# One hybrid decoder layer on one core: v's transposes and the first state-space unit later, the first norm's root on token columns, GELU on ACT and DVE, the last tiles by halves

## Chip, cores and metric

The kernel runs on one core of a Trainium2 chip, as one program. The metric is the device time of that core in microseconds, the median of several executions. The profile shows one execution: its span goes from the first to the last instruction that is recorded, and its own time is 1.8 us more than the span.

## What is computed

One inference step of one layer, for a prompt of 512 tokens and 8 single tokens of a sample group, which makes T = 520 columns of D = 1024 features:

```python
h = rmsnorm(x, g_mix)
z = h @ w_in          # u (512) | SWA q, k, v | three dilated q, k, v | three gates (3 x 1024)
a = gelu_glu(ssm(u))                    # branch A: complex diagonal state space, 32 groups x 64 states
b = banded_attention(q, k, v, sink)     # branch B
c = dilated_attention(...)              # branch C: keys by strides 1, 4, 16
x = x + (sigmoid(g_a) * (a @ w_a) + sigmoid(g_b) * (b @ w_b) + sigmoid(g_c) * (c @ w_c)) @ w_out
x = x + relu(rmsnorm(x) @ w_up) ** 2 @ w_down
x = x + sigmoid(rmsnorm(x) @ w_pg) * (p @ w_pp)
y = rmsnorm(x)
```

All of it is in float32. The new key and value rows and the state of the state space are outputs too. The change leaves this as it is; GELU is the form with tanh, in which `y (1 + 0.044715 y^2)` is now written as `0.044715 y (1 / 0.044715 + y^2)`.

## The kernel before

**Projections.** The activations lie transposed: features in partitions (8 tiles of 128, k = 0 to 7), tokens in columns, cut into half 0 (columns 0 to 255) and half 1 (256 to 519: 264 columns). One tile f of a projection is 128 output features; for each half it is a *half tile* of 24 matmuls, since float32 is rebuilt from three passes in fp32r for each k: high weight by high activation (`wh`, `hh`, L282), high by low (`hl`, L283), low by high (`wl`, L284). `load_w` brings a weight in pieces of 256 KB with a DMA of SyncE's queue (SP, L267); ACT rounds it to `wh` (L270) and DVE subtracts to get `wl` (L271). Four `wh` and `wl` slots and five raw ones are in turn; a weight can only be rounded when the piece four before has been used for the last time. `load_w` has a second set of two slots for a pool of its own, used for `w_pp`. PSUM has a ring of three `mm` banks and four `aux` banks, and single banks `stat` and `saux`.

**Order.** Each engine runs its own queue in order. The program is written as one sequence, which a scheduler then rearranges within its dependencies. Where in the sequence side work stands is set by *lanes*: after each half tile `tick()` lets every lane take a step (class `Lane`). Lane 0 computes the state space's parameters (`ssm_steps`: many small DVE and POOL operations, at the end eight pairs of tables `a2`, the powers, L618 to L626, each sent to `esc` by a DMA). The lane `att` holds attention and the transposes of v, `ssml` the eight units of the state space. A unit has eleven stages, in which `None` is an empty one: loads, tables (POOL computes X and others, L729 to L743), inputs, blocks (PE L761 and L763 on X), turned, windows, chunks, scan, None, states, outputs (to DRAM). The second argument of the lane is the gap: a unit begins five ticks after the one before.

**The stretches the change touches.** *Start*: SP issues x's parts and the first two weights in turn (`take`, W01); ACT makes `hh` (L347) and the squares of x (L417). `first_norm` sums the squares over features with a matmul with ones (L450), one column for each token in all 128 partitions, and `inverse` forms 1/sqrt on tiles of 128x256 and 128x264: ACT's root (L367) and five DVE operations (L368 to L372), the reciprocal among them. Each projection is multiplied by this when it is evacuated (`u` L678 and L679, `qkv` L877 to L882). *v_tokens* (L890) transposes v, 128x128 a time, in the step after its projection. *GELU*: in the branch b, at tiles f = 2 to 5, y comes from DRAM; POOL forms y + 0.044715 y^3 in three operations (L1369 to L1371), ACT takes the tanh (L1372), DVE multiplies (L1373, L1376), ACT and DVE split the product (`gh` L292, `gl` L296). *End*: the last product is the gate's. `tiles` hands out the half tiles as `TURNS` lists them; here the last four are (6, 1), (7, 1), (6, 0), (7, 0), each 24 matmuls and 6 of `w_pp`. DVE forms x (L1487, L1488), ACT its square (L307) and the scaled copy `yo` (L1493). After f = 7 of a half comes the final norm: sums on token columns (L340), for half 1 `newton` (three DVE operations, then twelve of POOL, L355 to L362), for half 0 a root on ACT and `root_inverse` (L367 to L372). `spread` turns the columns to rows: diagonals `nd` (L1497 by ACT, L1501 by DVE), a matmul with ones (L389) and a copy (L391). DVE and POOL multiply `yo` by it (L1506, L1504), and DMAs take it out (L1508). A table load on ACT (L1491) gets the square root back in the last tile.

Of the kernel before, what the change touches and what calls it, by code (L numbers as in the profile page):

```python
# [10 lines left out]
F32 = mybir.dt.float32  # L11
# [187 lines left out]
def body(tc, nc, I, O):  # L199
# [61 lines left out]
    def load_w(src, nk, pool=None, ks=None, lo_by=None):  # L261
        out = []
        pl, sfx, nb = (wp, "", 4) if pool is None else (pool, "p", 2)
# [87 lines left out]
    def newton(ps, n, on):  # L351

        nt = ev.tile([128, 4, 3], F32, name="nt", bufs=2)[:, :, :n]
        v, w, y, t = (nt[:, i] for i in range(4))
        V.tensor_scalar(v, ps, 1.0 / D, EPS, op0=OP.mult, op1=OP.add)  # L355
        V.tensor_scalar(y.bitcast(I32), v.bitcast(I32), -0.5, float(0x5f3759df), op0=OP.mult, op1=OP.add)
        V.tensor_scalar(w, v, -0.5, None, op0=OP.mult)
        for _ in range(3):
            on.tensor_tensor(t, w, y, op=OP.mult)
            on.tensor_tensor(t, t, y, op=OP.mult)  # L360
            on.tensor_scalar(t, t, 1.0, 1.5, op0=OP.mult, op1=OP.add)
            on.tensor_tensor(y, t, y, op=OP.mult)  # L362
        return y
# [17 lines left out]
    def spread(y, half, on):  # L381

        pr = stat()
# [45 lines left out]
    for k0, n, w in ((0, 2, 0), (2, 2, 4), (4, 4, None)):  # L429
        do = take(0, k0, n)  # L430
        if w is not None:
            W01[0] += load_w(I["w_in"][0], 8, ks=[w])
        do()
    for k0 in (0, 4):
        do = take(1, k0, 4)
        W01[1] += load_w(I["w_in"][1], 8, ks=[k0])
        do()
# [8 lines left out]
    def first_norm():  # L446
        for half, bank_ in enumerate((stat, aux)):
            c0, c1 = HALVES[half]
            ps = bank_()[:, :c1 - c0]
            PE.matmul(ps, ones, sq0[:, 0, c0:c1], start=True, stop=True)  # L450
            Rr[half] = inverse(ps)
# [238 lines left out]
    def ssm_sub(s):  # L690
# [145 lines left out]
        ssml.add(loads, tables, inputs, blocks, turned, windows, chunks, scan, None, states, outputs)  # L836
# [152 lines left out]
    def dilated(gi, f0, perm, name, Vt, i):  # L989
# [6 lines left out]
        att.add(v_tokens(Vt[i], v))  # L996
# [187 lines left out]
    for i in (4, 5, 0, 1, 2, 3):  # L1184
# [3 lines left out]
        if i == 5:  # L1188
            Vs = qt("vs")[:, 0:512].rearrange("p (b c) -> p b c", b=4)
            att.add(v_tokens(Vs, ts[5]))  # L1190
# [172 lines left out]
    def gelu(f):  # L1363
        def do():
# [4 lines left out]
            G.tensor_tensor(t, y, y, op=OP.mult)  # L1369
            G.tensor_scalar(t, t, 0.044715, 1.0, op0=OP.mult, op1=OP.add)  # L1370
            G.tensor_tensor(t, t, y, op=OP.mult)  # L1371
            A.activation(t, t, AF.Tanh, scale=math.sqrt(2.0 / math.pi))  # L1372
# [44 lines left out]
    def tiles(load, swap=False):  # L1417
        for t in TURNS:
            if swap and len(t) == 4:
                t = [(f, 1 - half) for f, half in t]  # L1420
# [62 lines left out]
    for f, half, (W, Wy) in tiles(lambda f: (load_w(I["w_pg"][f], 8), load_w(I["w_pp"][f], 2, pe)), swap=True):  # L1483
# [5 lines left out]
        if (f, half) == (7, 0):  # L1489

            A.activation(pe.tile([128, 1], F32, name="root"), t[:, 0:1], AF.Sqrt, scale=0.0, bias=ones[:, 0:1])  # L1491
        add_square(x, f, half, A, True, wide=False)
        A.activation(yo[:, f, c0:c1], x[:, f, c0:c1], AF.Copy, scale=prm[:, P_GF + f:P_GF + f + 1])  # L1493
        if f == 7:
            n = len(starts(half))
            if half:
                r, pr_ = spread(newton(ssp_[half][:, :n], n, G), half, lambda d, i, y: A.activation(d, i, AF.Copy, scale=y))  # L1497
            else:
                nt = ev.tile([128, 3, 2], F32, name="nr", bufs=1)
                y = root_inverse(ssp_[half][:, :n], *(nt[:, i] for i in range(3)))  # L1500
                r, pr_ = spread(y, half, lambda d, i, y: V.tensor_scalar(d, i, y, None, op0=OP.mult))  # L1501
            for k in range(8):
                if k in ((1, 2, 3, 5, 7) if half else (2, 5, 7)):
# [3 lines left out]
                if k % 2:  # L1507
                    (nc.sync if k in (1, 5) else nc.scalar).dma_start(O["yT"][:, k - 1:k + 1, c0:c1], yo[:, k - 1:k + 1, c0:c1])  # L1508
# [42 lines left out]
```

## Time and profile before

| | before |
|---|---|
| median of 3 runs | 1007.12 us (1006.59 to 1007.61) |
| profiled execution, its own time | 1006.62 us |
| its span | 1004.8 us |
| mean granted TensorE clock | 0.986 of full |
| PE busy (matmuls) | 974.3 us, 97% |
| PEld, weight loads, beside PE | 938.4 us, 93% |
| DVE busy | 622.0 us, 62% |
| ACT busy | 380.4 us, 38% |
| POOL busy | 247.3 us, 25% |

How to read it: the share of PE is an average; 30.5 us of its span are idle, in few places. The granted clock is the share of TensorE's full clock that the chip gave; it has two levels, 1.00 (2.4 GHz) and 0.50 (1.2 GHz), and a mean between them says how a stretch is divided. A busy PE at the lower level is busy for longer with the same work.

### The profile page before, as it was taken

Reading aid. Unit: us, or ns where it says so; the run is one execution under the profiler, and the core shown is the slowest. Engines: PE = TensorE matmul, PEld = TensorE weight load, DVE = VectorE, ACT = ScalarE, POOL = GpSimd, SP = SyncE. Lnnn points to the kernel's source line nnn. Section 1 sums busy time; section 2 is a strip of 40 time slices with the busy share of each in tenths; the row PEclk is TensorE's granted clock in tenths of the full one; section 3 lists DMA queues with packets and bytes.
Section 4 is the critical chain, followed back from the end, with each engine's and each line's share of the span. In section 5 each row is a group of like instructions: output and inputs, shape, how many; then the busy total and the mean of one; then the engine's idle time right before and its main releaser. Section 6 shows DMA issues by size and latency. Waiting matters only on the chain.

```text
span 1004.8 us, 20850 instructions
## 1 busy us (share of the span) xinstructions
PE 974.3 (97%) x8076; PEld 938.4 (93%) x8076; DVE 622.0 (62%) x1489; ACT 380.4 (38%) x845; POOL 247.3 (25%) x392
## 2 busy tenths in 40 slices
PE   7988899999999999999999999999999999999994
PEld 7988789988788999999999999999999999999994
DVE  7998556565988585566666844533543444366863
ACT  6323233342445443353344533322332233145652
POOL 0267855545531062100000132300320121000003
PEclk9999899999999999999999999999999999999997
DMA  6536544346322153352332232232232232232402
GB/s 227 174 107 205 150 120 127 97 117 190 117 70 62 50 153 95 93 170 86 95 105 86 85 102 88 91 99 86 93 98 85 95 95 84 85 106 86 147 12 85
DMA packets 80051, 108.46 MB, mean 108 GB/s; under 512 B 20432, under 2 KB 35920, under 8 KB 79952
## 3 DMA queue, kind: packets, MB, share of 16 engines
q1 hardware_dynamic: 78144, 105.64, 33.7%
q10 hardware_dynamic: 1808, 1.49, 0.5%
q8 instruction: 63, 1.03, 0.4%
q14 instruction: 36, 0.29, 0.1%
HBM read 97.04 MB, written 10.07 MB: 107 GB/s over the span
## 4 chain that ended last, share of the span: by engine, by line
PE 84%; DVE 6%; POOL 4%; DMA 2%; ACT 2%; issue 1%; POOLq 0%; SPq 0%; DVEq 0%
PE mm L282 21%; PE mm L284 21%; PE mm L283 21%; PE aux L282 4%; PE aux L284 4%; PE aux L283 4%; PE aux L906 2%; PE aux L931 1%; PE aux L964 1%; DVE wl L271 1%; PE aux L1240 1%; PE saux L827 1%; PE saux L828 1%; PE saux L788 1%; DMA bct<-bc 1%
## 5 line engine op out<-in xcount | busy, mean ns | idle before, releaser
L282 PE MATMUL mm<-hh,wh 128*128 128x256 f32 (+1 forms) x1072 | 306.7, 286 | 4.3 <-ACT wh L270 3.5
L284 PE MATMUL mm<-hh,wl 128*128 128x256 f32 (+1 forms) x1072 | 304.9, 285 | 0.2 <-DVE wl L271 0.2
L283 PE MATMUL mm<-hl,wh 128*128 128x256 f32 (+1 forms) x1072 | 304.2, 284 | 0.4 <-DVE hl L348 0.4
L270 ACT ACTIVATE wh<-wr 128x512 fp32r<-128x512 f32 (+1 forms) x292 | 181.2, 624 | 309.1 <-PE mm L283 243.4
L271 DVE TENSOR_TENSOR wl<-wr,wh 128x512 fp32r<-128x512 f32 (+1 forms) x290 | 210.5, 727 | 131.2 <-ACT wh L270 123.3
L282 PEld LDWEIGHTS mm<-hh,wh 128*128 128x128 f32 x1072 | 202.8, 189 | 8.1 <-ACT wh L270 3.8
L284 PEld LDWEIGHTS mm<-hh,wl 128*128 128x128 f32 x1072 | 203.1, 189 | 2.3 <-issue 1.8
L283 PEld LDWEIGHTS mm<-hl,wh 128*128 128x128 f32 x1072 | 203.0, 189 | 2.0 <-issue 1.4
L282 PE MATMUL mm<-rh,wh 128*128 128x256 f32 (+1 forms) x512 | 144.9, 283 | 0.0
L284 PE MATMUL mm<-rh,wl 128*128 128x256 f32 (+1 forms) x512 | 144.6, 282 | 0.0
L283 PE MATMUL mm<-rl,wh 128*128 128x256 f32 (+1 forms) x512 | 144.4, 282 | 0.0
L1450 POOL TENSOR_TENSOR e<-e 128x256 f32<-128x256 f32 x64 | 54.9, 859 | 350.1 <-DVE e L1449 279.5
L282 PE MATMUL aux<-hh,wh 128*128 128x264 f32 (+1 forms) x400 | 115.7, 289 | 1.6 <-ACT wh L270 1.6
L284 PE MATMUL aux<-hh,wl 128*128 128x264 f32 (+1 forms) x400 | 114.3, 286 | 0.6 <-DVE wl L271 0.6
L283 PE MATMUL aux<-hl,wh 128*128 128x264 f32 (+1 forms) x400 | 113.8, 285 | 0.0
L284 PEld LDWEIGHTS mm<-rh,wl 128*128 128x128 f32 x512 | 96.5, 189 | 0.0
L283 PEld LDWEIGHTS mm<-rl,wh 128*128 128x128 f32 x512 | 96.5, 188 | 0.0
L282 PEld LDWEIGHTS mm<-rh,wh 128*128 128x128 f32 x512 | 96.4, 188 | 0.0
L282 PEld LDWEIGHTS aux<-hh,wh 128*128 128x128 f32 x400 | 75.8, 190 | 3.9 <-issue 1.8
L284 PEld LDWEIGHTS aux<-hh,wl 128*128 128x128 f32 x400 | 75.9, 190 | 1.5 <-DVE wl L271 1.2
L283 PEld LDWEIGHTS aux<-hl,wh 128*128 128x128 f32 x400 | 76.1, 190 | 0.1
L1458 DVE TENSOR_TENSOR x<-mm,x 128x256 f32<-128x256 f32 (+1 forms) x64 | 27.4, 428 | 50.9 <-PE mm L284 50.9
(501 smaller groups left out, 1622.2 us busy)
## 6 DMA issues: line engine op xcount, KB each, us to landing
wr<-w_in SPq DMA_DIRECT2D x104, 256.0 KB, 3.1
wr<-w_up SPq DMA_DIRECT2D x64, 256.0 KB, 2.7
wr<-w_down SPq DMA_DIRECT2D x64, 256.0 KB, 2.6
wr<-w_out SPq DMA_DIRECT2D x16, 256.0 KB, 2.6
wr<-w_pg SPq DMA_DIRECT2D x16, 256.0 KB, 2.7
dkv<-kd SPq DMA_DIRECT2D x3, 1024.0 KB, 5.5
dkv<-vd SPq DMA_DIRECT2D x3, 1024.0 KB, 5.6
out_kv<-qkv SPq DMA_DIRECT2D x8, 260.0 KB, 2.3
```

The source lines that it names most:

```text
L270: A.activation(hi[:, :n], raw[:, :n], AF.Copy)
L271: (lo_by or V).tensor_tensor(lo[:, :n], raw[:, :n], hi[:, :n].bitcast(F32), op=OP.subtract)
L282: PE.matmul(ps, wh, ah[:, k, c0:c1], start=k == 0, stop=False)
L283: PE.matmul(ps, wh, al[:, k, c0:c1], start=False, stop=False)
L284: PE.matmul(ps, wl, ah[:, k, c0:c1], start=False, stop=k == n - 1)
L788: PE.matmul(xa[:, g], z["BL"][:, g], z["U"][:, g, 8:80], start=True, stop=True)
L827: PE.matmul(py[:, g], z["T2"][:, g].rearrange("p h t -> p (h t)"), z["U"][:, g, 0:72], start=True, stop=False)
L828: PE.matmul(py[:, g], z["CL"][:, g].rearrange("p h t -> p (h t)"), z["S_"][:, g, 0:72], start=False, stop=True)
L906: PE.matmul(ps[g][:, e, k0:k1], q, k, start=True, stop=True)
L931: PE.transpose(pt[:, at:at + 128], s_[:, e, c * 128:c * 128 + 128], ident)
L1450: G.tensor_tensor(t, t, t, op=OP.mult)
L1458: V.tensor_tensor(x[:, f, c0:c1], ps, x[:, f, c0:c1], op=OP.add)
```

## The change

Eight edits:

- The second weight's two pieces (W01[1]) are issued ahead of both parts of x's half 1.
- `first_norm` sums squares with the tokens in partitions (two columns of 128x1 for half 0, three for half 1), takes the inverse root on 128x2 and 128x3, and gets the rows back by `spread` (diagonals by ACT, L453; matmul L387; copy L389).
- `newton` runs on DVE alone, with four operations of each round written as three; both halves use it at the end. The table load for the root goes.
- The first unit of the state space gets two empty stages before inputs and two before blocks, and a gap of nine.
- The transposes of v come two steps later.
- GELU's POOL operations become a Square on ACT and one operation on DVE, and a factor moves into the tanh's scale.
- The last product takes tiles 0 to 3 by both halves, then half 1 of 4 to 7, then half 0 of 4 to 7; the weights of f = 6 and 7 lie in a pool of their own, and the second set of slots has four.
- POOL takes six instead of five of half 1's last multiplications, and all output DMAs of half 1 go to SP's queue.

```diff
-        pl, sfx, nb = (wp, "", 4) if pool is None else (pool, "p", 2)
+        pl, sfx, nb = (wp, "", 4) if pool is None else (pool, "p", 4)
...
-    def newton(ps, n, on):
+    def newton(ps, n):
...
-            on.tensor_tensor(t, w, y, op=OP.mult)
-            on.tensor_tensor(t, t, y, op=OP.mult)
-            on.tensor_scalar(t, t, 1.0, 1.5, op0=OP.mult, op1=OP.add)
-            on.tensor_tensor(y, t, y, op=OP.mult)
+            V.tensor_tensor(t, w, y, op=OP.mult)
+            V.tensor_tensor(t, t, y, op=OP.mult)
+            V.scalar_tensor_tensor(y, t, 1.5, y, op0=OP.add, op1=OP.mult)
...
-    def spread(y, half, on):
-        pr = stat()
+    def spread(y, half, on, pr):
...
+    W01[1] = load_w(I["w_in"][1], 8)
     for k0 in (0, 4):
-        do = take(1, k0, 4)
-        W01[1] += load_w(I["w_in"][1], 8, ks=[k0])
-        do()
+        take(1, k0, 4)()
...
-            c0, c1 = HALVES[half]
-            ps = bank_()[:, :c1 - c0]
-            PE.matmul(ps, ones, sq0[:, 0, c0:c1], start=True, stop=True)
-            Rr[half] = inverse(ps)
+            n = len(starts(half))
+            ps = bank_()
+            ssp_[half] = ps[:, 0:n]
+            for i, a in enumerate(starts(half)):
+                c0 = HALVES[half][0] + a
+                PE.matmul(ps[:, i:i + 1], sq0[:, 0, c0:c0 + 128], ones[:, 0:1], start=True, stop=True)
+            nt = ev.tile([128, 3, 3], F32, name="nr", bufs=2)[:, :, :n]
+            y = root_inverse(ssp_[half], *(nt[:, i] for i in range(3)))
+            Rr[half] = spread(y, half, lambda d, i, y: A.activation(d, i, AF.Copy, scale=y), ps)[0]
...
-        ssml.add(loads, tables, inputs, blocks, turned, windows, chunks, scan, None, states, outputs)
+        late = [None, None] if s == 0 else []
+        ssml.add(loads, tables, *late, inputs, *late, blocks, turned, windows, chunks, scan, None, states, outputs,
+                 gap=5 + 2 * len(late))
...
-        att.add(v_tokens(Vt[i], v))
+        att.add(None, None, v_tokens(Vt[i], v))
...
-            G.tensor_tensor(t, y, y, op=OP.mult)
-            G.tensor_scalar(t, t, 0.044715, 1.0, op0=OP.mult, op1=OP.add)
-            G.tensor_tensor(t, t, y, op=OP.mult)
-            A.activation(t, t, AF.Tanh, scale=math.sqrt(2.0 / math.pi))
+            A.activation(t, y, AF.Square)
+            V.scalar_tensor_tensor(t, t, 1.0 / 0.044715, y, op0=OP.add, op1=OP.mult)
+            A.activation(t, t, AF.Tanh, scale=0.044715 * math.sqrt(2.0 / math.pi))
...
+    LAST = [[(f, 0), (f, 1)] for f in range(4)] + [[(f, half) for half in (1, 0) for f in (4, 5, 6, 7)]]
...
-    for f, half, (W, Wy) in tiles(lambda f: (load_w(I["w_pg"][f], 8), load_w(I["w_pp"][f], 2, pe)), swap=True):
+    pe7 = sp(R, "pe7", side="right")
+    for f, half, (W, Wy) in tiles(lambda f: (load_w(I["w_pg"][f], 8, pe7 if f > 5 else None),
+                                             load_w(I["w_pp"][f], 2, pe)), LAST):
...
-        if (f, half) == (7, 0):
-            A.activation(pe.tile([128, 1], F32, name="root"), t[:, 0:1], AF.Sqrt, scale=0.0, bias=ones[:, 0:1])
...
+            r, pr_ = spread(newton(ssp_[half][:, :n], n), half,
+                            lambda d, i, y: V.tensor_scalar(d, i, y, None, op0=OP.mult), stat())
...
-                if k in ((1, 2, 3, 5, 7) if half else (2, 5, 7)):
+                if k in ((0, 1, 2, 3, 5, 7) if half else (2, 5, 7)):
```

**Where the instructions moved.** Three places, first before, then now; a row names line, operation and output <- inputs, and the line numbers of the new kernel are 2 less to 4 more.

ACT, at the start (`hh` of half 0 and 1, squares `sq0`, and `wh` with its raw weight `wr`):

```order
L347 ACTIVATE hh_92<-x0_81,prm_82 128x256 x4
L417 ACTIVATE sq0_100<-x0_81 128x4x256
L347 ACTIVATE hh_92<-x0_81,prm_82 128x264 x4
L417 ACTIVATE sq0_100<-x0_81 128x4x264
L270 ACTIVATE wh_147<-wr_145 128x512
L347 ACTIVATE hh_92<-x0_81,prm_82 128x264 x4
```
```order
L347 ACTIVATE hh_92<-x0_81,prm_82 128x256 x4
L415 ACTIVATE sq0_100<-x0_81 128x4x256
L270 ACTIVATE wh_146<-wr_144 128x512
L270 ACTIVATE wh_152<-wr_150 128x512
L347 ACTIVATE hh_92<-x0_81,prm_82 128x264 x4
L415 ACTIVATE sq0_100<-x0_81 128x4x264
```
The second weight's two pieces (145 and, later, 160 before; 144 and 150 now) stand ahead of half 1's first four `hh`.

PE, at the first transposes of v (L890, now L894), among the half tiles of the projections:

```order
L282 MATMUL mm<-hh,wh 128x264
L283 MATMUL mm<-hl,wh 128x264
L890 MATMUL aux<-cst,qkv 128x128 x4
L284 MATMUL mm<-hh,wl 128x264
L282 MATMUL mm<-hh,wh 128x264
```
```order
L283 MATMUL mm<-hl,wh 128x256
L284 MATMUL mm<-hh,wl 128x256
L894 MATMUL aux<-cst,qkv 128x128 x4
L282 MATMUL aux<-hh,wh 128x264
L283 MATMUL aux<-hl,wh 128x264
```
Counted in three-pass matmuls, the transposes stood 26 behind the last one of their projection (24 the next two times), and now stand 72 behind it.

DVE, at the last of the powers (a2, L626, now L628; `qkv_1428` is the eighth projection, `qkv_1231` now the sixth, `qkv_1335` the seventh):

```order
L877 TENSOR_TENSOR qkv_1428<-mm_1345,ny_321 128x4x64
L626 SCALAR_TENSOR_TENSOR a2_1112<-a1_1111 128x256
L1043 TENSOR_SCALAR Sx_512<-aux_1370,cst_85 128x128
L1059 COPY Sx_512<-aux_1379 128x1
L623 TENSOR_SCALAR a2_1129<-a1_1128 128x256
L1045 SCALAR_TENSOR_TENSOR Sx_512<-aux_1370,cst_85,Sx_512 128x128
L624 TENSOR_SCALAR a2_1129<-a2_1129 128x256
L1045 SCALAR_TENSOR_TENSOR Sx_512<-aux_1370,cst_85,Sx_512 128x128 x2
L626 SCALAR_TENSOR_TENSOR a2_1129<-a1_1128 128x256
```
```order
L882 TENSOR_TENSOR qkv_1231<-aux_1206,ny_351 128x4x64
L883 TENSOR_TENSOR qkv_1231<-aux_1206,ny_351 128x8
L626 TENSOR_SCALAR a2_1141<-a2_1141 128x256
L271 TENSOR_TENSOR wl_1348<-wr_1345,wh_1347 128x512
L628 SCALAR_TENSOR_TENSOR a2_1141<-a1_1140 128x256
L881 TENSOR_TENSOR qkv_1335<-aux_1254,ny_333 128x4x64
```
The last power has moved from behind the eighth projection's evacuation to behind the sixth's.

## Rows read from the trace of the kernel before

**Rows 1.** The page, part 1: engine, busy us (share of the span), instructions.
```profile
PE 974.3 (97%) x8076; PEld 938.4 (93%) x8076; DVE 622.0 (62%) x1489; ACT 380.4 (38%) x845; POOL 247.3 (25%) x392
```
**Rows 2.** Waits of PE: line <- releaser, us in total, times, longest us.
```profile
PE aux L890 <- DVE qkv L878: 5.3, 2, 3.0
```
**Rows 3.** Windows: PE, PEld, DVE, ACT, POOL busy (instructions), clock, DMA share, GB/s.
```profile
15.00:20.00 5.00, 5.00 (x31) 4.88 (x30) 5.00 (x16) 3.56 (x8) 0.00 (x0) 0.69 0.25 85
25.00:50.00 25.00, 25.00 (x209) 24.93 (x208) 23.64 (x94) 7.90 (x13) 5.98 (x9) 1.00 0.53 176
50.00:100.00 50.00, 44.49 (x364) 42.71 (x363) 45.29 (x119) 15.93 (x31) 34.82 (x55) 1.00 0.45 155
```
**Rows 4.** Windows behind the first block's wait and behind the last GELU's.
```profile
107.30:113.70 6.40, 6.36 (x44) 5.30 (x45) 5.36 (x15) 2.82 (x6) 6.32 (x9) 0.50 0.57 167
378.90:383.30 4.40, 4.08 (x19) 3.88 (x20) 3.16 (x7) 1.84 (x4) 1.30 (x1) 0.62 0.45 134
```
**Rows 5.** Timeline, ACT and PE at the start: start us, us, engine, line, operation [idle before <- releaser].
```profile
11.04 1.72 ACT L347 ACTIVATE hh<-x,prm 128x264 fp32r<-128x264 f32 x4
...
13.64 0.62 ACT L270 ACTIVATE wh<-wr 128x512 fp32r<-128x512 f32 x1
...
14.30 0.39 PE L282 MATMUL mm<-hh,wh 128*128 128x256 f32 x1 [2.77 <-ACT wh L270]
...
25.04 0.61 PE L450 MATMUL aux<-sq,ones 128*128 128x264 f32 x2
```
**Rows 6.** Timeline, DVE in the first norm's inverse.
```profile
20.44 1.74 DVE L369 RECIPROCAL ny<-nw 128x256 f32<-128x256 f32 x1
...
26.43 0.41 DVE L371 TENSOR_TENSOR nw<-nw,ny 128x256 f32<-128x256 f32 x1
```
**Rows 7.** Timeline, PE in the final norm of half 1.
```profile
989.85 0.71 PE L389 MATMUL stat<-nd,ones 128*128 128x264 f32 x2 [1.49 <-ACT nd L1497]
...
990.40 0.50 PE L340 MATMUL stat<-ones,ssq 128*128 128x1 f32 x4
```
**Rows 8.** Timeline, the branch b with GELU: DVE, POOL, ACT and PE.
```profile
357.16 0.68 DVE L271 TENSOR_TENSOR wl<-wr,wh 128x512 fp32r<-128x512 f32 x1
...
358.41 3.02 POOL L1371 TENSOR_TENSOR yt<-yt,y 128x520 f32<-128x520 f32 x2
...
358.44 1.83 DVE L271 TENSOR_TENSOR wl<-wr,wh 128x512 fp32r<-128x512 f32 x1
...
377.69 0.64 ACT L292 ACTIVATE gh<-g 128x520 fp32r<-128x520 f32 x1 [1.81 <-DVE g L1376]
...
378.90 0.39 PE L282 MATMUL aux<-hh,wh 128*128 128x256 f32 x1 [1.64 <-ACT wh L270]
```
**Rows 9.** Timeline, the tail: DVE, ACT and POOL behind PE's last half tile.
```profile
989.05 0.42 DVE L1488 SCALAR_TENSOR_TENSOR x<-e,x 128x256 f32<-128x256 f32 x1
989.81 1.28 ACT L1491 ACT_TABLE_LOAD   x1
...
991.31 0.40 ACT L307 ACTIVATE e<-x 128x256 f32<-128x256 f32 x1
...
992.46 3.53 POOL L1504 TENSOR_TENSOR yo<-yo,ny 128x264 f32<-128x264 f32 x5 [3.58 <-ACT ny L391]
...
993.70 0.22 DVE L370 TENSOR_TENSOR nr<-nr 128x2 f32<-128x2 f32 x1
993.95 0.66 DVE L371 TENSOR_TENSOR nr<-nr 128x2 f32<-128x2 f32 x1
...
994.65 0.66 DVE L372 SCALAR_TENSOR_TENSOR nr<-nr 128x2 f32<-128x2 f32 x1
995.34 0.92 DVE L1501 TENSOR_SCALAR nd<-cst,nr 128x128 f32<-128x128 f32 x2
```
**Rows 10.** Timeline, POOL's last power and PE at the first block.
```profile
95.73 0.74 POOL L625 TENSOR_TENSOR a<-a,a 128x256 f32<-128x256 f32 x1 [1.41 <-DVE a L624]
...
107.34 0.31 PE L761 MATMUL saux<-C,X 128*32 128x16 f32 x8 [3.54 <-POOL X L731]
```

More of the change, by code (lines that the diff above doesn't have):

```diff
@@ L1189, in body @@
             Vs = qt("vs")[:, 0:512].rearrange("p (b c) -> p b c", b=4)
-            att.add(v_tokens(Vs, ts[5]))
+            att.add(None, None, v_tokens(Vs, ts[5]))
     ob = hl(po, "ob", 4)
@@ L1415, in body, with tiles @@
     TURNS = [[(f, 0), (f, 1)] for f in range(6)] + [[(6, 0), (7, 0), (6, 1), (7, 1)]]
[L1417 to L1420, printed above, removed]
+    LAST = [[(f, 0), (f, 1)] for f in range(4)] + [[(f, half) for half in (1, 0) for f in (4, 5, 6, 7)]]
+    def tiles(load, turns=TURNS):
+        for t in turns:
             Ws = {f: load(f) for f in sorted({f for f, _ in t})}
@@ L1495, in body @@
             n = len(starts(half))
[L1496 to L1501, printed above, removed]
+            r, pr_ = spread(newton(ssp_[half][:, :n], n), half,
+                            lambda d, i, y: V.tensor_scalar(d, i, y, None, op0=OP.mult), stat())
             for k in range(8):
-                if k in ((1, 2, 3, 5, 7) if half else (2, 5, 7)):
+                if k in ((0, 1, 2, 3, 5, 7) if half else (2, 5, 7)):
                     G.tensor_tensor(yo[:, k, c0:c1], yo[:, k, c0:c1], r, op=OP.mult)
@@ L1507, in body @@
                 if k % 2:
-                    (nc.sync if k in (1, 5) else nc.scalar).dma_start(O["yT"][:, k - 1:k + 1, c0:c1], yo[:, k - 1:k + 1, c0:c1])
+                    (nc.sync if half or k in (1, 5) else nc.scalar).dma_start(O["yT"][:, k - 1:k + 1, c0:c1], yo[:, k - 1:k + 1, c0:c1])
     R.close()
```

## Prediction

> **What bounds the kernel now.** I read the page first, then PE's waits, the windows, and the timeline around each wait. TensorE is busy 974.3 us of 1004.8 [rows 1], so an edit counts for what it takes from PE's 30.5 us of idle time, or from time in which PE ran at the lower granted clock; anywhere else it costs what it adds to PE. Four places hold the waits outside the tail: 2.77 us at the start, for the high part of a weight [rows 5]; 5.3 at the transposes of v [rows 2]; 3.54 at the first state-space block, for X [rows 10]; 1.64 at the last GELU, again for a weight [rows 8]. Two prices recur. At a granted clock of 1.00 PE issues a matmul each 25.00 / 209 = 0.120 us [rows 3]. In 15 to 20 us it got 31 where 42 fit, at a mean clock of 0.69 [rows 3]: 11 x 0.12 = 1.3 us lost for 5 x (1 - 0.69) = 1.55, so a microsecond at 0.50 (the 1.2 GHz level) costs about 0.43. The clock fell after the waits of 2.77, 3.54 and 1.64 us [rows 3, 4]; after the two at L890 (3.0 and 2.3) the window of 50 to 100 still reads 1.00 [rows 2, 3]. So a wait can cost more than its length, and I count the second part only where a row shows it. DVE is busy 23.64 of 25 us from 25 to 50 and 45.29 of 50 from there to 100 [rows 3]: there it binds nearly as much as PE.
>
> **The change, part by part.** The sum is made against the profiled execution: span 1004.8, time 1006.62, so 1.8 us lie around the span; it is 0.5 us under the median 1007.12.
>
> *Start.* ACT makes the high part of the second weight tile only at 13.64, behind four hh of half 1 (1.72 us from 11.04) and a square; PE stands 2.77 us until 14.30, and the clock falls [rows 5]. Now SP issues both pieces ahead of x's second half, and ACT takes them at 11.04. PE can go on at about 11.7, with two small waits for DVE's low parts, 0.3 to 0.9 together, by the 0.68 of one L271 [rows 8]. ACT's last hh then ends at about 16.6 (11.04, two weights 1.1, hh 1.7, a square 1.0, hh 1.7), and PE's first 96 matmuls end near 21 instead of 25.04 [rows 5]. Gained: 2.8 of idle and 1.3 of clock, less 0.5 of new waits: **3.6**, bounds 2.5 to 4.1.
>
> *First norm.* DVE loses two chains of five wide operations, 2 x 1.74 + 8 x 0.41 = 6.8 us [rows 6], and gets ten on 2 or 3 columns, 0.22 each by L370 in the tail [rows 9]: 4.6 less. PE gets five one-column sums in two passes each (10 x 0.125 = 1.25, from the four in 0.50) and two spreads (2 x 0.71) and loses two wide sums (0.61 and about as much) [rows 5, 7]: 1.4, of which I take **1.1** as not overlapped, bounds 0.5 to 1.5. ACT's five diagonals and two copies stand in its queue before the weights of the fifth tile; PE reaches the first spread 26 matmuls (3.1 us) after the second sum, against some 2.5 for root and diagonals. So I cost that wait at nothing, with a cover of about half a microsecond.
>
> *v later, and DVE.* In the order before, L890 stands 26 matmuls behind the end of its projection; with a wait of 3.0, DVE's evacuation ended 26 x 0.12 + 3.0 = 6.1 us after the projection. Now 72 matmuls lie between, 8.6 us, so L894 should not wait: 5.3 us go. But DVE still has 69 us of work in these 75 [rows 3], less 4.6, and PE now wants to cross the stretch about 10 us sooner. What is late next is the low part of weights (L271), queued on DVE behind the same evacuations. Between 0 and 5.3 I take **2.6**, the middle: 64 us of work fit into 65 only without gaps.
>
> *First block.* PE stops 3.54 us for X; POOL's last power of the tables began at 95.73, and X was there at 107.3, 11.6 us later (a DMA out, one back, seven POOL operations) [rows 10]. In DVE's order the last power now follows the evacuation of the sixth projection instead of the eighth's: four half tiles, 4 x 24 x 0.12 = 11.5 us earlier, so X comes near 96. PE came at 107.34 - 3.54 = 103.8 and now comes 3.6 - 1.1 + 2.6 = 5.1 sooner, at 98.7, with eight score matmuls ahead of the block. The wait goes with some 3 us to spare, and with it the clock of 0.50 from 107.3 to 113.7 (6.4 x 0.43 = 2.7) [rows 4]: **6.2**, bounds 3 to 6.3. The two empty stages and the gap of 9 put the later units' matmuls 20 to 55 matmuls further back; the last still comes before the end of the attention: nothing.
>
> *GELU.* The last gh holds ACT's queue until 377.69, 1.81 us for DVE's g, with the next weight behind it; PE waits 1.64, and in the 4.4 us behind it the clock reads 0.62 [rows 4, 8]: 19 matmuls where 36 fit, 2.1 us by that count, 1.4 by the clock (4.4 x 0.38 x 0.85). POOL's three products for one f (the third 1.5 us each) become one ACT Square, taken as gh's 0.64, and one DVE operation of about 0.7. The chain of one f gets more than 2 us shorter. 1.64 and about 2: **3.6**, bounds 1.5 to 3.8; the lower one since the Squares wait for y's DMA ahead of weights in ACT's queue.
>
> *Tail.* x is done at 989.47, but its square starts at 991.31, because the table load (1.28 us) and its root lie between [rows 9]: 1.8 us. From the square's end, 991.71, to the diagonal at 995.34 went 3.6 us, for the sums on PE, a root and five operations, two of them 0.66 beside POOL; now the sums and 12 dependent operations at 0.22 take 1.0 + 2.6: the same. The diagonal, 0.92 beside POOL, may need 0.5: 0.4. For output of half 1 that leaves earlier I guess 0.1. **2.3**, bounds 0 to 3.2. POOL loses its part of half 1's Newton, which now lies beside PE's last tiles.
>
> *Weights of the last tiles.* By halves, W of f = 5 takes slots that the tile before frees, one half tile (30 matmuls, 3.6 us) ahead of its need; ACT and DVE need 0.6 + 0.7 for a piece [rows 8]. Covered.
>
> **Sum:** 3.6 - 1.1 + 2.6 + 6.2 + 3.6 + 2.3 = 17.2; 1006.6 - 17.2 = **989.4** is my forecast; against the median that is 18 less.
>
> **Rivals.**
> 1. *DVE binds from 20 to 100 us.* For it: 92% busy now [rows 3], and PE comes earlier. Then the 2.6 becomes nothing, the start's gain is returned as waits for low parts down to about 1, and one stretch of the lower clock (about 2) is added: 989.4 + 2.6 + 2.6 + 2 = 996.6. Against it: 4.6 us less work there.
> 2. *POOL in the tail.* Half 1's six products (3.53 / 5 = 0.71 each [rows 9]) now start about 2.5 us before PE's end, and DVE's last tile and Newton meet them: five operations at 0.66 instead of 0.22 and the diagonal again at 0.92, 2.6 in all: the tail gains nothing, 991.7. The two operations at 0.66 and the 1.83 us of a low part beside POOL's products, against 0.68 [rows 8, 9], bear it out.
> The Trainium skill (SBUF — State Buffer, who interferes with whom) has this as a rule: a DVE operation with two SBUF inputs and a POOL operation that reads SBUF exclude each other, and the later waits for all of the other. The rows agree with it.
> 3. *X still late.* POOL's X stands behind copies of q that wait for the seventh projection's evacuation; if those come 6 us late, as at L890, and the DMA back too, the 6.2 stays: 995.6.
> 4. *Slower.* One mechanism: DVE's low parts late in each of the projection tiles f = 4 to 9, each a wait of 1.7 us with 2 of lower clock behind it, as at the GELU. Six of these cost 22, more than the sum: 1011. It decides from five such tiles on. Against it: the two long waits at L890 left the clock at 1.00.
> 5. *The change doesn't do what it says.* A scheduler rewrites the order, so v's move and the unit's delay could be lost; but in the order L894 does stand 46 matmuls further back. If only start, GELU and tail came: 1006.6 - 3.6 - 3.6 - 2.3 = 997.1.
>
> **Chances.** Forecast (986 to 992.5) 0.50; rival 1, alone or in part, 0.23; rival 2 0.10, inside the range; rival 3 0.07; rival 5 0.05; rival 4 0.03; all bounds at their good end (22.2 us, 984.4) or better 0.02. The range takes 984 to 997.5 and leaves out some 1 in 8. A measurement of this kernel can tell about 0.2%, 2 us, from no change; only rival 4 and a bad mixture of 1, 3 and 5 reach there: faster 0.94, same 0.03, slower 0.03.
>
> **What would show it.** Right: no PE wait for wh before 20 us and the second sum near 21; no wait at L894 and L763 and a granted clock of 1.00 from 25 to 125; none at the GELU; no table load after the last tile, and the last square within 0.3 us of x. Wrong: PE waits for L271 or an evacuation in 25 to 100, or a clock under 0.95 there; a wait at the first spread (L387); POOL's yo beside DVE's Newton at the end. A result above 997.5 would say that DVE's stretch, not the named waits, set the time.

## The result, and the profile after

| | before | changed |
|---|---|---|
| median | 1006.86 us (1005.59 to 1007.61, 4 runs) | 991.68 us (989.51 to 993.04, 4 runs) |
| profiled execution, its own time | 1006.62 us | 992.71 us |
| its span | 1004.8 us | 990.9 us |
| mean granted TensorE clock | 0.986 | 0.993 |

The ratio is 0.9849, with an interval of 0.9826 to 0.9872: 1.5% or 15 us faster, and 2.3 us short of the forecast. First the page of the changed kernel, which answers to [rows 1]: PE was idle for 25.8 us of its span (990.9 - 965.1), 4.7 less than before, and its busy time fell by 9.2 us.

```profile
span 990.9 us, 20857 instructions
PE 965.1 (97%) x8086; PEld 931.5 (94%) x8086; DVE 619.7 (63%) x1511; ACT 379.7 (38%) x850; POOL 230.2 (23%) x369
```

Four of the waits of PE in the changed kernel (us in total, times, longest), which answer to [rows 2]. The waits for X, for the transposes of v and for the last GELU are gone. A new one of 3.6 us stands at the top, for an evacuation by DVE, and two lines with 4.7 us for low parts (L271).

```profile
PE mm L282 <- DVE e L1322: 3.6, 1, 3.6
PE aux L284 <- DVE wl L271: 2.4, 3, 1.1
PE mm L284 <- DVE wl L271: 2.3, 5, 1.0
PE mm L282 <- ACT whp L270: 0.6, 1, 0.6
```

To see where the time came from I cut both spans at the same instructions: *mark a* is the start of DVE's fifth addition to M in the branch b, *mark b* the last gate before the product behind the GELU, *mark c* the 41st addition to x of the down projection, *mark d* the last x of all. Where a stretch holds the same matmuls in both kernels, it is the same work.

| stretch | before | changed | difference | predicted |
|---|---|---|---|---|
| start to a | 350.69 | 338.30 | -12.4 | -11.3 (start, first norm, v, first block) |
| a to b (GELU) | 46.57 | 42.45 | -4.1 | -3.6 |
| b to c (from the product behind the GELU into the third down product) | 464.97 | 463.37 | -1.6 | 0 |
| c to d (rest of the down products, last product) | 126.82 | 133.29 | +6.5 | 0 |
| d to the end | 15.75 | 13.49 | -2.3 | -2.3 |
| span | 1004.8 | 990.9 | -13.9 | -17.2 |

From mark c to the last addition to x of the down projection it takes 68.04 us in both kernels (862.23 to 930.27, 844.12 to 912.16), so the 6.5 us are lost in the last product.

Windows of the kernel before for two of these stretches, and for 20 us of its last product (length; then PE, PEld, DVE, ACT and POOL busy with their instructions; the granted clock; DMA share; GB/s):

```profile
350.69:397.26 46.57, 44.62 (x357) 44.21 (x356) 32.62 (x58) 18.34 (x35) 21.39 (x19) 0.96 0.42 123
397.26:862.23 464.97, 464.97 (x3870) 464.85 (x3869) 245.61 (x485) 161.85 (x316) 61.60 (x73) 1.00 0.31 97
940.00:960.00 20.00, 20.00 (x168) 20.00 (x168) 16.95 (x42) 12.66 (x31) 0.00 (x0) 1.00 0.27 88
```

The same two stretches in the changed kernel, and below them the windows that answer to [rows 3] and one of the last product:

```profile
338.30:380.75 42.45, 42.45 (x357) 42.45 (x356) 32.13 (x61) 20.31 (x39) 5.60 (x7) 1.00 0.47 135
380.75:844.12 463.37, 463.37 (x3870) 463.25 (x3869) 245.80 (x484) 161.62 (x316) 61.62 (x73) 1.00 0.31 97
15.00:20.00 5.00, 5.00 (x44) 5.00 (x44) 5.00 (x19) 4.32 (x10) 0.00 (x0) 1.00 0.42 154
25.00:50.00 25.00, 24.03 (x196) 23.42 (x194) 23.59 (x107) 7.54 (x15) 11.08 (x12) 1.00 0.44 148
50.00:100.00 50.00, 46.57 (x371) 44.09 (x372) 40.95 (x91) 16.65 (x32) 36.42 (x64) 1.00 0.51 166
930.00:936.00 6.00, 5.93 (x37) 5.96 (x38) 4.31 (x11) 3.01 (x9) 0.00 (x0) 0.72 0.02 3
```

Three things are to be seen. Around the GELU PE is busy from end to end, and the clock stays at 1.00 where it was 0.96. From b to c 3870 matmuls run without a gap and at 1.00 in both kernels, and still take 1.60 us less; no edit touches them. And in 930 to 936 us PE gets 37 matmuls where 50 fit, at a clock of 0.72: part of the stretch is at the lower level. The kernel before reads 1.00 from 940 to 960 us, in its last product.

The timeline of the changed kernel around the places of [rows 5, 10] (start, us, engine, line, operation [idle before <- releaser]). ACT has the second weight at 11.57 instead of 13.64, PE waits 0.17 and 0.31 us there, and half 1's sums come at 22.18 instead of 25.04. POOL's last operation on X starts at 95.86, and PE comes to the first block at 103.31, without a wait:

```profile
11.57 1.14 ACT L270 ACTIVATE wh<-wr 128x512 fp32r<-128x512 f32 x2
12.24 0.39 PE L282 MATMUL mm<-hh,wh 128*128 128x256 f32 x1 [0.17 <-ACT wh L270]
13.05 0.38 PE L284 MATMUL mm<-hh,wl 128*128 128x256 f32 x1 [0.31 <-DVE wl L271]
22.18 0.83 PE L450 MATMUL aux<-ones,sq 128*128 128x1 f32 x6
95.86 0.77 POOL L733 TENSOR_TENSOR X<-X,t 128x64 f32<-128x64 f32 x1
103.31 0.26 PE L763 MATMUL saux<-C,X 128*32 128x16 f32 x8
```

The new stall, at the start of the last product (DVE's rows of the changed kernel, and PE's after them). The inverse of the norm of half 1 is five operations, L367 to L371. Between the reciprocal and the next of them DVE makes five low parts (`wlp`, 2.8 us). Four are 128x512, the pieces of f = 6 and 7; the fifth, 128x256, is one of `w_pp` (the row of three shows the form of its first). Then the low parts of two more pieces come between. The evacuation (L1322) needs `ny`, and PE needs the bank that it frees:

```profile
921.54 1.79 DVE L368 RECIPROCAL ny<-nw 128x264 f32<-128x264 f32 x1
923.25 1.22 DVE L271 TENSOR_TENSOR wlp<-wrp,whp 128x512 fp32r<-128x512 f32 x2
924.72 1.62 DVE L271 TENSOR_TENSOR wlp<-wrp,whp 128x512 fp32r<-128x512 f32 x3
926.26 0.43 DVE L369 TENSOR_TENSOR nw<-nw,ny 128x264 f32<-128x264 f32 x1
926.94 1.29 DVE L271 TENSOR_TENSOR wl<-wr,wh 128x512 fp32r<-128x512 f32 x2
929.02 0.43 DVE L371 SCALAR_TENSOR_TENSOR ny<-nw,ny 128x264 f32<-128x264 f32 x1
929.49 0.43 DVE L1322 TENSOR_TENSOR e<-mm,ny 128x264 f32<-128x264 f32 x1
930.07 0.55 PE L282 MATMUL mm<-hh,wh 128*128 128x256 f32 x1 [3.57 <-DVE e L1322]
```

The tail of the changed kernel, which answers to [rows 9]. The last x takes 1.01 us beside POOL's six products where it took 0.42; the square follows it by 0.1 us, with no table load; two of the twelve operations of `newton` are shown, at 0.16 us each, spaced by 0.20:

```profile
973.42 4.73 POOL L1502 TENSOR_TENSOR yo<-yo,ny 128x264 f32<-128x264 f32 x6 [153.47 <-ACT ny L389]
977.41 1.01 DVE L1493 SCALAR_TENSOR_TENSOR x<-e,x 128x256 f32<-128x256 f32 x1
978.52 0.42 ACT L307 ACTIVATE e<-x 128x256 f32<-128x256 f32 x1 [1.60 <-DVE x L1493]
979.63 0.16 DVE L355 TENSOR_SCALAR nt<-stat 128x2 f32<-128x2 f32 x1 [1.21 <-PE stat L340]
981.66 0.16 DVE L361 SCALAR_TENSOR_TENSOR nt<-nt 128x2 f32<-128x2 f32 x1
981.86 0.48 DVE L1499 TENSOR_SCALAR nd<-cst,nt 128x128 f32<-128x128 f32 x2
```

### The profile page after: what moved, and what is told of

Same layout as the page of the kernel before. It is cut to its first block, busy times and chain, and to the rows that moved or that the text cites. A ratio compares the mean times of both kernels' runs of the same rounds, so it can differ in the third digit from the quotient of the medians.

```text
span 990.9 us, 20857 instructions
## 1 busy us (share of the span) xinstructions
PE 965.1 (97%) x8086; PEld 931.5 (94%) x8086; DVE 619.7 (63%) x1511; ACT 379.7 (38%) x850; POOL 230.2 (23%) x369
## 4 chain that ended last, share of the span: by engine, by line
PE 89%; DVE 5%; DMA 2%; issue 1%; POOL 1%; ACT 1%; SPq 0%; POOLq 0%; ACTq 0%; DVEq 0%
PE mm L282 22%; PE mm L283 22%; PE mm L284 22%; PE aux L282 5%; PE aux L283 5%; PE aux L284 5%; PE aux L910 2%; PE aux L935 1%; PE aux L968 1%; DVE wl L271 1%; PE aux L1244 1%; PE saux L830 1%; PE saux L829 1%; PE saux L790 1%; POOL yo L1502 1%
## 5 line engine op out<-in xcount | busy, mean ns | idle before, releaser
L282 PE MATMUL mm<-hh,wh 128*128 128x256 f32 (+1 forms) x1040 | 296.9, 286 | 5.2 <-DVE e L1322 3.6
L284 PE MATMUL mm<-hh,wl 128*128 128x256 f32 (+1 forms) x1040 | 295.2, 284 | 2.4 <-DVE wl L271 2.3
L283 PE MATMUL mm<-hl,wh 128*128 128x256 f32 (+1 forms) x1040 | 296.0, 285 | 0.5 <-DVE hl L348 0.4
L271 DVE TENSOR_TENSOR wl<-wr,wh 128x512 fp32r<-128x512 f32 (+1 forms) x286 | 209.4, 733 | 129.5 <-ACT wh L270 120.3
L270 ACT ACTIVATE wh<-wr 128x512 fp32r<-128x512 f32 (+1 forms) x288 | 178.5, 624 | 290.9 <-PE mm L283 236.3
L282 PEld LDWEIGHTS mm<-hh,wh 128*128 128x128 f32 x1040 | 196.5, 189 | 10.4 <-issue 7.1
L284 PEld LDWEIGHTS mm<-hh,wl 128*128 128x128 f32 x1040 | 196.2, 189 | 4.1 <-DVE wl L271 3.6
L283 PEld LDWEIGHTS mm<-hl,wh 128*128 128x128 f32 x1040 | 196.4, 189 | 3.2 <-issue 2.2
```

Of the source, the lines that this page charges most:

```text
L270: A.activation(hi[:, :n], raw[:, :n], AF.Copy)
L271: (lo_by or V).tensor_tensor(lo[:, :n], raw[:, :n], hi[:, :n].bitcast(F32), op=OP.subtract)
L282: PE.matmul(ps, wh, ah[:, k, c0:c1], start=k == 0, stop=False)
L283: PE.matmul(ps, wh, al[:, k, c0:c1], start=False, stop=False)
L284: PE.matmul(ps, wl, ah[:, k, c0:c1], start=False, stop=k == n - 1)
```

## Experiments

Experiments 1 to 10 are single executions. On the same chips the kernel before took 1007.69 us beside the first four, 1010.08 beside the next four, and a median of 1007.49 (8 runs, 1004.29 to 1008.44) beside the last. Five executions with the same edits ahead of mark a (the changed kernel twice, experiments 1, 7 and 11) came to it between 336.39 and 339.00. So a difference of 2.6 us at a, between two executions, can be chance. Distances at a below are given from the profiled changed kernel (338.30) or from the kernel before (350.69).

**1. The raw tiles of the last weights from the common ring.** My theory for the stall: the pool of their own lets the weights of f = 6 and 7 be made as soon as their DMAs land, ahead of the norm on DVE's queue.

```diff
-            raw = pl.tile([128, 4, 128], F32, name="wr" + sfx, bufs=nb + 1)
+            raw = wp.tile([128, 4, 128], F32, name="wr", bufs=5) if nk == 8 else \
+                pl.tile([128, 4, 128], F32, name="wr" + sfx, bufs=nb + 1)
```

> The raw tiles of the last product's f = 6 and 7 come from the common ring of five, so that these weights are made when their turn comes and not at the product's start; all else as in the changed kernel. Theory (DVE made four low parts of 128x512 for these tiles in front of the norm of half 1, and the bank that PE wanted was freed 3.6 us late): the wait of PE for the evacuation at the start of the last product (3.57 us in the changed kernel) falls under 0.5, the clock from 926 to 950 reads 1.00 instead of 0.93, and the profiled time is 5 us shorter (4 to 6.5): near 987.5. Rival (the wide inverse of half 1 and the table load are late by themselves, and the weights only fill their gaps): the wait stays above 2.5 us, and the time within 1.5 us of 992.7.

987.23 us. With raw tiles that come in turn with the others, the last weights are loaded later, and one low part, of `w_pp`, is left between the reciprocal and the next operation. The window of 930 to 936 in this kernel:

```profile
930.00:936.00 6.00, 6.00 (x52) 6.00 (x52) 5.62 (x13) 4.76 (x11) 0.00 (x0) 1.00 0.40 131
```

and DVE's rows of the norm, some 10 us earlier (its line numbers are one higher):

```profile
920.41 1.80 DVE L369 RECIPROCAL ny<-nw 128x264 f32<-128x264 f32 x1
922.39 0.42 DVE L272 TENSOR_TENSOR wlp<-wrp,whp 128x256 fp32r<-128x256 f32 x1
922.72 0.43 DVE L370 TENSOR_TENSOR nw<-nw,ny 128x264 f32<-128x264 f32 x1
923.87 0.43 DVE L372 SCALAR_TENSOR_TENSOR ny<-nw,ny 128x264 f32<-128x264 f32 x1
```

PE waits nowhere there, and no clock is lost. At mark c the two kernels are 0.17 us apart, at d 5.95 (977.41 and 971.46): the early weights cost 5.8, of which 4.2 are waits (3.57 and 0.59). It holds over all runs, though the size changes: in the seven executions with the early weights (the changed kernel twice, experiments 2 to 6) PE waits 2.9 to 3.6 us for this evacuation, and c to d takes 130.73 to 133.33 us; in the three without (1, 7 and 11) there is no such wait, and it takes 127.37 to 127.51.

**2. v's transposes in the next step, as before.**

```diff
-        att.add(None, None, v_tokens(Vt[i], v))
+        att.add(v_tokens(Vt[i], v))
...
-            att.add(None, None, v_tokens(Vs, ts[5]))
+            att.add(v_tokens(Vs, ts[5]))
```

> v's transposes again in the step after their projection, all else as in the changed kernel. Theory (the two empty steps took away the waits at the transposes, and DVE's other waits are not made of the same time): waits of PE for the evacuation of 2 to 3 us come back, and the half tiles from 100 us on stand 2 to 5 us later than in the changed kernel. Rival (DVE binds from 25 to 80, so the time of the waits only changes its name): the waits at the transposes come back, those for the low parts of weights (3.8 us in 43 to 77 now) shrink by as much, and the half tiles after 100 us stand within 1 us.

1002.56 us, and 9.9 us behind the changed kernel at mark a (348.24). Its waits of PE:

```profile
PE aux L894 <- DVE qkv L882: 6.0, 2, 3.6
PE mm L284 <- DVE wl L271: 3.5, 5, 1.5
```

The wait is back, somewhat longer than before the change [rows 2], and here it does cost clock: 0.93 from 50 to 75 us. With a wait of 1.53 for a low part at 290 us, and a clock of 0.69 behind it, that makes 10 us, twice what I expected, from an edit that takes at most some 2 off the kernel before (9, below).

**3. The first unit without its empty stages.**

```diff
-        late = [None, None] if s == 0 else []
+        late = []
```

> The first unit of the state space without its four empty stages and with the gap of five, all else as in the changed kernel. Theory (the empty stages are what covers X now): PE comes to the first block some 96 matmuls, or 11 us, earlier in its order, waits 2 to 5 us for X, the clock falls, and the half tiles after 120 us stand 4 to 8 us later. Rival (the lighter DVE alone has brought X early enough): no wait at the block above 0.5 us, and the half tiles within 1 us of the changed kernel's.

1002.0 us, 9.0 us behind at mark a (347.29). POOL's last operation on X starts at 95.17, as early as in the changed kernel; PE is there at 89.6 and stands:

```profile
95.55 0.31 PE L763 MATMUL saux<-C,X 128*32 128x16 f32 x8 [5.92 <-POOL X L733]
```

The clock is 0.74 from 89 to 102 us. So the empty stages do not make X earlier; they bring PE to it later.

**4. The first norm on wide tiles, as before** (`first_norm` alone).

```diff
-            n = len(starts(half))
...
-            Rr[half] = spread(y, half, lambda d, i, y: A.activation(d, i, AF.Copy, scale=y), ps)[0]
+            c0, c1 = HALVES[half]
+            ps = bank_()[:, :c1 - c0]
+            PE.matmul(ps, ones, sq0[:, 0, c0:c1], start=True, stop=True)
+            Rr[half] = inverse(ps)
```

> The first norm's root again on 128x256 and 128x264, all else as in the changed kernel. Theory (DVE is nearly the bound there, and loses 4.6 us by the columns): waits of PE for low parts and evacuations in 20 to 80 us grow by 2 to 5 us, less the 1.1 us of PE's own work that goes: half tiles from 100 us on 1 to 4 us later. Rival (DVE's idle 7% takes it in): half tiles 0.5 to 1.5 us earlier, for PE's work alone.

994.22 us, 2.5 behind at mark a (340.78). The wide root of half 0 stands on DVE ahead of the sum of squares of half 1, PE waits for that sum, which my theory did not name, and the clock from 25 to 50 us is 0.89:

```profile
24.79 1.25 PE L447 MATMUL aux<-sq,ones 128*128 128x264 f32 x2 [3.22 <-DVE sq L421]
```

From b to c this kernel takes 464.86 us: the 1.6 us are not there (8 says why).

**5. GELU by POOL, as before.**

```diff
-            A.activation(t, y, AF.Square)
-            V.scalar_tensor_tensor(t, t, 1.0 / 0.044715, y, op0=OP.add, op1=OP.mult)
-            A.activation(t, t, AF.Tanh, scale=0.044715 * math.sqrt(2.0 / math.pi))
+            G.tensor_tensor(t, y, y, op=OP.mult)
+            G.tensor_scalar(t, t, 0.044715, 1.0, op0=OP.mult, op1=OP.add)
+            G.tensor_tensor(t, t, y, op=OP.mult)
+            A.activation(t, t, AF.Tanh, scale=math.sqrt(2.0 / math.pi))
```

> GELU's first three operations on POOL again, all else as in the changed kernel. Theory (POOL's chain made the last gh late, ACT's queue held the next weight, and the clock fell): PE waits 1.5 to 2.5 us at the last GELU, the clock falls in the 5 us behind, and the half tiles from 385 us on stand 3 to 4.5 us later than in the changed kernel. Rival (the GELU starts earlier against PE now, so POOL would have been in time): no wait over 0.5 us, half tiles within 1 us.

992.13 us. The stretch from a to b:

```profile
338.20:383.14 44.94, 42.93 (x357) 42.52 (x356) 32.04 (x58) 18.31 (x35) 21.70 (x19) 1.00 0.41 128
```

The wait for the weight is back (1.69 us at 366.41, for ACT's `wh`), with 0.32 for its low part, but the clock stays at 1.00, against my theory. 44.94 - 42.45: GELU without POOL is worth 2.5 us here, 2.0 of it PE's idle time, and 4.1 in the profiled execution of before, where the clock fell as well. The profiled executions of 8 and 9, which have GELU as before, agree with the 2.5: 44.91 and 45.06 us from a to b, at 1.00.

**6. The second weight between the parts of x, as before.**

```diff
-    W01[1] = load_w(I["w_in"][1], 8)
...
-        take(1, k0, 4)()
+        do = take(1, k0, 4)
+        W01[1] += load_w(I["w_in"][1], 8, ks=[k0])
+        do()
```

> The second weight's pieces again between the parts of x's half 1, all else as in the changed kernel. Theory: PE waits 2.8 us at 11 to 14 us, the clock in 15 to 20 reads about 0.7, and the sums of half 1 end 2.5 to 3.5 us later than the changed kernel's 22.2; of this 1 to 3 us are left at 100 us and to the end. Rival (DVE binds from 25 to 80 us, so the start's gain is only waited away there): the half tiles after 100 us within 0.7 us of the changed kernel's.

992.2 us. The wait of the start is back (3.04 us for `wh` at 14.35), with a clock of 0.66 from 15 to 20, and the sums of half 1 come at 25.14, as before. But at mark a it is only 2.1 us behind (340.36): PE comes later into the stretch in which it waits for DVE, and waits there 2.6 us for low parts instead of 4.7.

**7. The last product as before** (order of the last tiles and their slots; `newton` on DVE stays).

```diff
-        pl, sfx, nb = (wp, "", 4) if pool is None else (pool, "p", 4)
+        pl, sfx, nb = (wp, "", 4) if pool is None else (pool, "p", 2)
...
-    LAST = [[(f, 0), (f, 1)] for f in range(4)] + [[(f, half) for half in (1, 0) for f in (4, 5, 6, 7)]]
+    LAST = [[(f, 0), (f, 1)] for f in range(6)] + [[(6, 1), (7, 1), (6, 0), (7, 0)]]
...
-    pe7 = sp(R, "pe7", side="right")
-    for f, half, (W, Wy) in tiles(lambda f: (load_w(I["w_pg"][f], 8, pe7 if f > 5 else None),
+    for f, half, (W, Wy) in tiles(lambda f: (load_w(I["w_pg"][f], 8),
```

> The last product in the order of before and with two slots for its second weights and no pool for f = 6 and 7; newton on DVE and all else as in the changed kernel. Theory (the early weights are the whole loss at the start of the last product, and half 1's earlier end is worth little): no wait at the start of the last product, 5 to 6 us gained there, and in the tail 0 to 2 us lost, since half 1's norm and products come closer to the end: profiled time 986.5 to 989.5. Rival (the order by halves is what shortened the tail): the tail is 4 us or more longer than with it, and the time above 991.

989.27 us, faster than the changed kernel. There is no stall at the start of the product, but half 1's output now meets the `newton` of half 0, whose rows show rival 2's price, 0.66 instead of 0.16:

```profile
973.11 4.23 POOL L1501 TENSOR_TENSOR yo<-yo,ny 128x264 f32<-128x264 f32 x6 [152.46 <-ACT ny L389]
976.00 0.66 DVE L360 TENSOR_TENSOR nt<-nt 128x2 f32<-128x2 f32 x1
978.18 0.16 DVE L360 TENSOR_TENSOR nt<-nt 128x2 f32<-128x2 f32 x1
```

From the last x to the end it takes 14.9 us (972.19 to 987.1), with the order by halves 13.6 (experiment 1: 971.46 to 985.1). So the halves are worth some 1.3 us, and the way in which their weights were loaded took back 6.

**8. The kernel before with a pad.** One tile of 96 bytes a partition that nobody uses is meant to move the activations `hh` and `hl` to the addresses that they have in the changed kernel. No view shows addresses; this is reckoned from the sizes of the tiles.

```diff
+    ev.tile([128, 24], F32, name="pad")
```

> The kernel before with 96 unused bytes in each partition, so that the activations (hh, hl, the branch's sums) lie at the addresses of the changed kernel; the instructions and their order stay. The changed kernel gains 1.7 us between 395 and 850 us, a little in every matmul and without any wait, and the kernel with the wide first norm does not. Theory (where the buffers lie sets a matmul's pitch by half a per cent in these stretches): half tiles here stand 1.2 to 2 us earlier at 850 us than before, in the same stretches. Rival (something else of the first norm's change): within 0.3 us of before everywhere.

1003.62 us. From b to c:

```profile
395.96:859.33 463.37, 463.37 (x3870) 463.25 (x3869) 245.87 (x485) 161.62 (x316) 61.69 (x73) 1.00 0.31 97
```

463.37 us, to the hundredth that of the changed kernel, with no other edit. Experiments 9 and 10, which have the tiles of before, take 464.97.

**9. Only v's transposes later** (the kernel before with both edits of experiment 2 the other way).

> The kernel before with v's transposes two steps later and nothing else. Theory (without the later unit, POOL's X still stops PE): the two waits at the transposes go (5.3 us before), but PE then comes to the first block earlier and waits there the longer (3.5 before, 6 to 9 now); half tiles after 355 us stand 0 to 2 us from before. Rival (each edit gives its own waits back): 4 to 5 us earlier.

1003.36 us, 1.9 us ahead of the kernel before at mark a (348.76), which is no more than the spread above. Waits of PE:

```profile
PE saux L761 <- POOL X L731: 3.5, 1, 3.5
PE aux L284 <- DVE wl L271: 2.9, 5, 0.8
PE mm L284 <- DVE wl L271: 0.6, 2, 0.4
```

The 5.3 us at the transposes become 3.5 for low parts, and X is as late as ever.

**10. Only the first unit later** (the kernel before with the empty stages and the gap).

> The kernel before with the first unit's four empty stages and its gap of nine and nothing else. Theory (the wait for X is cured by the empty stages alone): no wait at the first block and a clock of 1.00 from 100 to 125, the waits at the transposes stay (5.3); half tiles after 355 us 5 to 7 us earlier than before. Rival (waits move on to the next units or to the end of the attention): less than 3 us.

1002.29 us, again 1.9 us ahead at mark a (348.76). My theory, 5 to 7, missed; it is the rival's case. Waits of PE:

```profile
PE aux L892 <- DVE qkv L880: 5.1, 2, 2.8
PE saux L763 <- POOL CL L740: 1.1, 1, 1.1
PE saux L761 <- POOL X L731: 0.7, 1, 0.7
```

POOL's last operation on X starts at 106.8 here, at 107.0 before; PE comes 2.7 us later and waits for X and CL instead, and the clock falls all the same (0.93 from 75 to 125).

**11 and 12. The version without the stall, and the changed kernel, timed side by side.**

> The kernel with the paced weights, timed. Theory: 986 to 988 by the median, 2% less than before and 4 to 6 us less than the changed kernel beside it; its interval against the changed kernel's does not overlap. Rival (the one profile was a lucky execution): within 2 us of the changed kernel.

> The changed kernel itself, timed on the same chip as the one above: 990 to 993 by all theories; it is the other side of that comparison.

| | median | ratio to before |
|---|---|---|
| changed, raw tiles from the common ring | 987.51 us (986.49 to 988.01, 5 runs) | 0.9804 (0.979 to 0.9818) |
| changed | 992.54 us (990.39 to 993.08, 4 runs) | 0.9848 (0.9834 to 0.9862) |

The two do not overlap. The version without the early weights is faster than both kernels, 5 us under the changed one.

**What moved X.** Runs 3, 9 and 10 left a question: neither v's move nor the empty stages bring X forward. The last power of the tables has a place in DVE's queue, told by how many evacuations of the projections (`qkv`, two for each tile, one for each half) stand ahead of it:

| kernel | evacuations ahead of the last power | POOL's last operation on X starts at | PE's wait for X |
|---|---|---|---|
| before | 15 | 107.0 | 3.5 |
| only v later (9) | 15 | 106.5 | 3.5 |
| only the unit later (10) | 15 | 106.8 | 0.7 |
| changed, norm wide (4) | 13 | 99.5 | 0 |
| changed, weight between (6) | 11 | 98.2 | 0 |
| changed, unit soon (3) | 12 | 95.2 | 5.9 |
| changed, v soon (2) | 11 | 92.8 | 0 |
| changed | 12 | 95.9 | 0 |

Undoing any one of the four edits of this stretch leaves the place near 12, and v's move or the unit's delay alone leaves it at 15. So the start and the first norm are the likely movers, and with the other edits in place either is enough for most of it (4 and 6). No run has one of them alone on the kernel before, or v's move and the delay together, so this is not shown. The scheduler sets the place; no line of the change says so.

## Why the prediction was right, and where not

991.68 lies 2.3 us from the forecast and inside its range, but that it is so near is in part luck, since misses of both signs stand behind it: the terms up to the GELU brought 16.5 us where 14.9 were forecast, a drift of 1.6 was not foreseen, the tail was right in sum, and a stall of 6 was priced at nothing. The total is also the one that rival 2 gave (991.7), but not by its mechanism.

*Start.* 3.6 forecast; the sums of half 1 came 2.9 us earlier (25.04 to 22.18), and 3.7 in the second profiled execution (21.31). Undone alone it costs 2.1 at mark a (1.4 to 4.0 against the five executions), in the way that rival 1 had it: part of the gain is returned as waits for low parts.

*First norm.* Costed at 1.1 for what it adds to PE; undone alone it loses 2.5 (1.8 to 4.4 against the five), so by this run the edit is a gain and not a cost. I had booked DVE's 4.6 us less work in the next term, without asking what in the queue it would release: the square sum of half 1 (experiment 4). No wait at the first spread, as forecast.

*v later, and DVE.* L894 does not wait, as forecast, and low parts are late next, with 4.7 us in place of 5.3 [rows 2]. That is rival 1 in its first step; its second, a stretch at the lower clock, did not come: 1.00 from 25 to 100 us. DVE had 40.95 us of work in the window from 50 to 100, where it had 45.29 [rows 3].

*First block.* X was forecast near 96 and came at 95.86; PE was forecast at 98.7 and came at 103.3, since the empty stages put other matmuls ahead of the block. The mechanism held, and rival 3 (X still late) did not occur. But I took the position of the last power as given by the change as a whole; the runs show that neither v's move nor the empty stages set it, and point to the start and the norm. Together these terms gave 12.4 at mark a for 11.3, and they are no sum: v's move and the unit's each bring 1.9 or less alone, no more than chance can, and cost 9 to 10 when taken away from the whole (experiments 2, 3, 9 and 10). My reading, which fits these runs but which none isolates: each removes one of three things that hold PE at about the same time (DVE's evacuation at L890, X, the order in which PE meets the block), and PE goes at the pace of the last one left.

*GELU.* 3.6 forecast, 4.1 measured, 2.5 where the clock does not fall. The two parts, wait and clock, were the right ones; the upper bound of 3.8 was 0.3 too low.

*Weights of the last tiles. "Covered."* This step failed. I asked only whether a weight could be late, and not what it does when it is early. With a pool of their own, the last weights wait for no earlier piece, so their high and low parts enter ACT's and DVE's queues at the start of the product, where half 1's norm is the work that PE needs; their four low parts and one of `w_pp` stand in the middle of it, and PE waits 3.57 us for a bank. Experiment 1 takes the early raw tiles away, and 5.8 us come back, 5.0 by the medians of 11 and 12. With the 6.5 of the table for c to d, and the 1.1, 0.5 and 1.6 gained above the forecast in the three stretches ahead of it, the account closes: 989.4 + 6.5 - 3.2 = 992.7, the time of the profiled execution.

*Tail.* 2.3 forecast and measured (15.75 to 13.49), but as a sum of two misses. The table load's 1.8 (1.7 measured) and the diagonal's 0.4 came as forecast. Rival 2 came in part: the last x took 1.01 us instead of 0.42 beside POOL's products, 0.6 lost. But `newton` began after their end (973.42 + 4.73 = 978.15), so it ran at 0.16, where the forecast had 0.22: from the square to the diagonal it is 3.34 us instead of 4.03, 0.7 gained where nothing was forecast. Experiment 7 shows what a meeting costs. The Trainium skill (SBUF — State Buffer, who interferes with whom) has it as a rule that a DVE operation with two SBUF inputs and a POOL operation that reads SBUF exclude each other. The 1.01 and the 0.66 agree with it.

*Rival 4* (slower) needed five late low parts of 1.7 us with the lower clock behind each; there were eight, the longest 1.1, and the clock stayed at 1.00 from 25 to 100 us. *Rival 5* is refuted: each edit shows in the trace.

## What to carry to other kernels

A weight that is free to come early takes its place in the queues of the engines that prepare it; before slots are added, look at what stands behind it on each of them, above all at the start of a product, where a norm is on the path. Gains at waits that follow each other closely may not add one by one: ask which wait is left after each removal, and whether a scheduler's order moves with the edit. And cut both traces at the same instructions before explaining a difference: stretches of equal work show at once what no edit was meant to do.

## What the runs showed of the hardware

*Addresses.* The stretch from b to c, 3870 matmuls without a gap and at a clock of 1.00, took 464.97 us before and 463.37 with 96 bytes more in a pool ahead of the activations (experiment 8). Every kernel of the study had one of these lengths, or 464.86 (experiment 4). The gain is not the same everywhere. First the third up product and the second down product of the kernel before, then the same two in the changed kernel:

```profile
697.93:746.91 48.98, 48.98 (x410) 48.98 (x409) 24.47 (x50) 16.49 (x33) 13.53 (x16) 1.00 0.30 97
746.91:790.17 43.26, 43.26 (x362) 43.26 (x361) 16.80 (x30) 9.60 (x16) 0.00 (x0) 1.00 0.27 86
```
```profile
680.37:729.08 48.71, 48.71 (x410) 48.71 (x409) 24.49 (x50) 16.49 (x33) 13.81 (x16) 1.00 0.31 97
729.08:772.34 43.26, 43.26 (x362) 43.26 (x361) 16.81 (x30) 9.61 (x16) 0.00 (x0) 1.00 0.28 87
```

The up product reads `hh` and `hl`, which the pad moves; it is 0.27 us shorter. The down product reads `rh` and `rl`, from a pool that is laid out from the other side (`side="right"`), and is 43.26 us in every run. How an address does that is open. Whether it also acts ahead of mark a no run isolates: experiment 8 came to it 0.36 us later than the kernel before (351.05).

*The clock.* It fell after the wait of 1.64 us at the GELU [rows 4, 8], and not after 1.69 at the same place in experiment 5, nor after 1.67 in experiment 8, with the same matmuls around it (a to b in experiment 8):

```profile
351.05:395.96 44.91, 42.93 (x357) 42.52 (x356) 32.64 (x57) 18.32 (x35) 21.31 (x19) 1.00 0.42 128
```

So a wait's second part, the clock behind it, cannot be told from its length alone; in this kernel the same edit is worth 2.5 or 4.1 us by it.
